# A hybrid attention and gMLP layer on one core: the gate's transpose copied out of PSUM by the scalar engine, the key's transpose moved beside the query's

## The chip, the cores and the metric

The kernel runs on one core of a Trainium2 chip. The metric is the device time of one execution in microseconds. Engines are named as in the profile: PE (matrix products and transposes), DVE (vector engine), ACT (scalar engine), POOL (GpSimd) and SP, which here issues most of the transfers.

## The reference

One layer works on `x` of 4096 tokens by 1024 channels, all float32:

```
h = rms(x) * (1 + scale) + shift
q, k, v, g_attn, u, v_gm, g_gm = split(h @ w_in)
attn = windowed_gqa(q, k, v)            # +-128 tokens, 8 query heads on 2 key heads, ALiBi, sink
gm   = chunked_gmlp(u, v_gm)            # chunks of 128 tokens
y = concat([attn * silu(g_attn), gm * silu(g_gm)])
x = x + gate * (y @ w_out)
```

The change lies in `attn * silu(g_attn)`, and in the transposes of `k` and `q` that the scores need.

## The kernel before

The sequence is cut into 32 blocks of 128 tokens. Matrix products keep float32 accuracy by splitting each operand into a high and a low part and adding three products, so that every block costs 24 products for keys and values (`pk`, 256 columns), 24 for queries (`pq`, 512) and 24 for the gate (`pg`, 512). After a short start the first part of the program is a loop (L782) over iterations i = 3 to 34. `run_iter` (L684) walks through the main products of block i in the order `pk`, `pq`, `pg` (`mains1`, L186) and puts side steps among them, at positions between 0 and 1 that the table `TUNE` (L36 to L40) and `sides1` (L635 to L682) give; of equal positions the one added first comes first. The attention of block a = i - 3 is among the side steps. A second part computes the gMLP branch and the output product; the change does not touch it.

The table sets the order in which the steps are written. The framework's scheduler then orders the instructions of each engine, and starts from the written order; only in iterations 29 to 31 (`chained`) are PE's pinned to it.

The steps that matter here, in the order of an iteration:

- `load1` and `split1` (L96, L97): SP loads the next blocks' `xraw` (transposed) and `xtok` (by tokens); ACT casts `xraw` to the high part `xh`, POOL computes the low part `xl`.
- `qk` (L538), one step for each head: two score products into a tile of pool "s" (`s`, names s_0 to s_7), a DVE instruction that adds the mask and takes the row minimum (L551, the minimum lands in `mx`), and ACT's exponential (L555). After four heads `softmax` (L559) takes the exponential of the sink (`es`, L566), the sum, its reciprocal, and POOL scales the rows (L571).
- `silu1` (L527): ACT's tanh of the gate into the one buffer `th` (L531), then DVE's product (L536).
- `stats1` (L164): ACT squares `xtok` and sums the rows, DVE and POOL make the reciprocal root (L82, L83).
- `pt_` (L573): four transposes of probabilities into a bank of pool "t" (`pT`), ACT's cast to `ph` (L580), DVE's rest `pl` (L581), which reads the bank again. An iteration has six: two groups of heads by three key blocks, named pT_0_0 to pT_1_2. `pv_` (L584): the products with the values (`po`), ACT's copy `lo` (L598) and DVE's sums into `y` (L600).
- `tr_g` (L607): four transposes of the gate into a bank of pool "s" (`gT`). `finish1` (L602): DVE multiplies `y` by it (L604) and SP stores the result.
- `post_kv`, `post_q`, `post_g` (L432, L453, L493): DVE takes the products out of PSUM (`kvf` L437, `qf` L457, `gf` L495), ACT squares (L440, L460), DVE reduces (L467), POOL takes the power (L83), DVE multiplies (L470, L485, L491, L486).
- `tr_k` (L498) and `tr_q` (L508) for block i - 1: the transposed keys `pkT` into pool "t", with casts `kT` (L504, L505) and the rest (L506); the queries `pqT` into pool "s", with `qT` (L518, L519).

PSUM has four pools of two banks each (L108): "mm" for the main products, "s" for scores, `gT` and `pqT`, "t" for `pT` and `pkT`, "o" for `po`. The buffers of a pool are given out in turn, so a tile waits for the last reader of the tile that held its bank.

Of the kernel before, what the change touches and what calls it, by code (L numbers as in the profile page):

```python
# [8 lines left out]
F32 = mybir.dt.float32  # L9
# [7 lines left out]
P = 128  # L17
# [19 lines left out]
            "v2"], ["v3", "g2", "g3"]], wg0=1.05, wgd=0.18, vn=0, vx=0.2, wv0=0.145, wvd=0.15,  # L37
            silu=0.45, ksplit=2, sb=["q1", "g0", "g1", "q0", "q2", "g2"], ch0=28, load=0.02, split=0.0,
            stats=0.525, bg=0.1, qk0=0.08, qkd=0.035, pt0=0.485, ptd=0.0715, pvlag=0.31, trg=0.5,
            fin=0.99, trk=0.93, trq=0.9, order="kqg", unch=0, hp2=30, hpx=0, qeng="V")  # L40


def body(tc, x, xT, c, cT, w_adaT, b_adaT, w_gate, b_gate, ngT, w_in, q_gain, k_gain, sink, wsT, bsT, w_out, out):
    nc = tc.nc
    V, A, G, T = nc.vector, nc.scalar, nc.gpsimd, nc.tensor
# [17 lines left out]
    def tr(ps, src):  # L63
        pe(T.transpose(ps, src, ident))  # L64
# [56 lines left out]
    base = ctx.enter_context(tc.tile_pool(name="base", bufs=1))  # L121
# [485 lines left out]
    def tr_g(b):  # L607
        d = blk[b]
        pt = ps_s.tile([P, 4, P], F32, tag="s", name=f"gT{b}")
        for i in range(4):  # L610
            tr(pt[:, i], d["gf"][:, i * P : (i + 1) * P])
        d["pg"] = pt

    def bg_bias2(n):
        k, t = divmod(n, 3)
# [19 lines left out]
    def sides1(i):  # L635
# [17 lines left out]
        if 0 <= a < NB:  # L653
            for b in range(NB):
                if i == max(b + LAG - 1, NS):
                    add(TUNE["silu"] if b > 1 else 0.0, lambda b=b: silu1([b]))
            _, s0, s1 = slots(a)
            for h in range(NH):
                add(TUNE["qk0"] + TUNE["qkd"] * h, lambda h=h: qk(a, h))
            seq = [(j, q) for j in range(NKV) for q in range(s0, s1)]  # L660
            for n, (j, q) in enumerate(seq):
                add(TUNE["pt0"] + TUNE["ptd"] * n, lambda j=j, q=q: pt_(a, j, q))
                add(TUNE["pt0"] + TUNE["ptd"] * n + TUNE["pvlag"], lambda j=j, q=q: pv_(a, j, q))
            add(TUNE["trg"], lambda: tr_g(a))
            add(max(TUNE["fin"], TUNE["pt0"] + TUNE["ptd"] * 5 + TUNE["pvlag"] + 0.001), lambda: finish1(a))
# [535 lines left out]
```

## Time and profile before

| what | value |
|---|---|
| three runs | 1730.27, 1732.02 and 1732.11 us, median 1732.02 |
| the profiled execution | 1732.1 us, its span 1730.3 us |
| PE busy | 1661.7 us, 96% of the span |
| DVE, ACT, POOL busy | 1075.7, 738.7, 689.4 us |
| granted TensorE clock, mean over the span | 0.987 of full speed |
| the loop over blocks | steady from about 115 to 706 us, then a tail to about 870 us |

The span is the stretch that the profiler saw; the execution's time also has what lies around it, here 1.8 us. Busy time overlaps between engines. A wait of an engine is listed with the instruction that waited and the one that ended the wait; that of an engine off the critical path costs nothing.

### The profile page before, as it was taken

How to read it: one execution, taken by the hardware profiler on the slowest of the kernel's cores; microseconds unless marked ns; L12 is line 12 of the kernel's file. 1: busy time of each engine (PE TensorE's matmuls, PEld its weight loads, DVE VectorE, ACT ScalarE, POOL GpSimd, SP SyncE). 2: the span in 40 equal slices, each digit the busy share in tenths (PEclk: the TensorE clock that was granted, in tenths of full speed). 3: DMA queues.
4: the chain of work that ended last, by engine and by line, in shares of the span. 5: the costliest groups of instructions: out<-in, count | busy, mean ns of one | idle time of the engine just before them, and what ended most of it. 6: DMA issues, size and time to landing. Idle time of an engine off the chain costs nothing.

```text
span 1730.3 us, 23014 instructions
## 1 busy us (share of the span) xinstructions
PE 1661.7 (96%) x8216; PEld 1377.6 (80%) x8216; DVE 1075.7 (62%) x2279; ACT 738.7 (43%) x1613; POOL 689.4 (40%) x610
## 2 busy tenths in 40 slices
PE   6789999999999999998989999999999989999999
PEld 4578888888888888886778888887888877888887
DVE  7987777787777778779773333344443466444443
ACT  3476666666666666665421212211122233222221
POOL 5653343433344433336522222222222337545552
PEclk9899999999999999999999999999999999999999
DMA  7522112222112222122250111213233146555442
GB/s 257 195 86 74 57 54 74 74 74 74 48 63 74 73 74 80 35 70 79 75 183 30 49 37 49 84 69 116 104 116 97 56 166 216 165 164 180 150 149 83
DMA packets 67762, 170.92 MB, mean 99 GB/s; under 512 B 8256, under 2 KB 8256, under 8 KB 67648
## 3 DMA queue, kind: packets, MB, share of 16 engines
q1 hardware_dynamic: 62896, 160.81, 27.8%
q10 hardware_dynamic: 4752, 8.65, 1.3%
q8 instruction: 64, 1.05, 0.2%
q14 instruction: 50, 0.41, 0.1%
HBM read 128.54 MB, written 40.89 MB: 98 GB/s over the span
## 4 chain that ended last, share of the span: by engine, by line
PE 76%; DVE 11%; DMA 2%; ACT 2%; issue 1%; POOL 1%; SPq 0%; DVEq 0%; POOLq 0%; ACTq 0%
PE pg L61 16%; PE pv L61 9%; PE pq L61 9%; PE pu L61 8%; PE oY L967 7%; PE oZ L967 5%; PE oX L967 5%; PE s L61 4%; PE pT L64 4%; PE po L61 3%; DVE y L600 3%; DVE pr L551 1%; PE sv L61 1%; PE pk L61 1%; DVE gf L495 1%
## 5 line engine op out<-in xcount | busy, mean ns | idle before, releaser
L97 POOL TENSOR_TENSOR xl<-xraw,xh 128x1024 fp32r<-128x1024 f32 x58 | 149.8, 2582 | 366.7 <-ACT xh L96 366.7
L571 POOL TENSOR_SCALAR pr<-pr,den 128x384 f32<-128x384 f32 (+1 forms) x256 | 146.4, 591 | 162.4 <-DVE vs L445 119.0
L555 ACT ACTIVATE pr<-pr,mx 128x384 f32<-128x384 f32 (+1 forms) x256 | 153.8, 601 | 61.0 <-DVE mx L551 60.2
L551 DVE CUSTOM_DVE_ANT_0 pr<-s,negd,nsink 128x384 f32<-128x384 f32 (+1 forms) x256 | 152.5, 607 | 11.7 <-PE s L61 6.2
L580 ACT CAST ph<-pT 128x512 fp32r<-128x512 f32 x188 | 109.6, 584 | 115.7 <-PE po L61 43.0
L61 PE MATMUL pu<-w2u,xh 128*128 128x512 f32 x480 | 149.2, 392 | 0.0
L61 PE MATMUL s<-kT,qT 128*128 128x384 f32 (+1 forms) x512 | 136.4, 348 | 12.8 <-DVE mx L551 11.0
L581 DVE TENSOR_TENSOR pl<-pT,ph 128x512 fp32r<-128x512 f32 x188 | 126.0, 685 | 15.6 <-ACT ph L580 15.6
L83 POOL TENSOR_TENSOR ssv<-ssv,mhalf 128x8 f32<-128x8 f32 x32 | 54.3, 1696 | 183.3 <-DVE ssv L82 183.1
L64 PEld LDWEIGHTS pT<-ident,pr 128*128 128x128 f32 x752 | 93.3, 140 | 34.8 <-POOL pr L571 6.8
L64 PE MATMUL pT<-ident,pr 128*128 128x128 f32 x752 | 115.7, 274 | 5.2 <-DVE pl L581 3.5
L61 PEld LDWEIGHTS s<-kT,qT 128*128 128x128 f32 x512 | 87.3, 190 | 32.9 <-DVE mx L551 19.5
L61 PEld LDWEIGHTS pu<-w2u,xh 128*128 128x128 f32 x480 | 90.9, 189 | 18.8
L96 ACT CAST xh<-xraw 128x1024 fp32r<-128x1024 f32 x61 | 64.1, 1050 | 91.1 <-PE pu L61 89.0
L61 PE MATMUL pg<-wgh,xl 128*128 128x512 f32 x232 | 98.7, 425 | 0.0
L61 PE MATMUL pg<-wgh,xh 128*128 128x512 f32 x232 | 98.5, 424 | 0.0
L61 PE MATMUL pu<-w2u,xl 128*128 128x512 f32 x240 | 94.2, 392 | 1.2 <-DVE xl L97 1.2
L61 PE MATMUL pq<-w1h,xh 128*128 128x512 f32 x232 | 94.2, 406 | 0.0
L61 PE MATMUL pq<-w1l,xh 128*128 128x512 f32 x232 | 93.9, 405 | 0.0
L61 PE MATMUL pq<-w1h,xl 128*128 128x512 f32 x232 | 92.0, 396 | 0.0
L61 PE MATMUL pg<-wgl,xh 128*128 128x512 f32 x232 | 91.8, 396 | 0.0
L230 DVE SCALAR_TENSOR_TENSOR vf<-pv,rstd,bias 128x512 f32<-128x512 f32 x32 | 24.0, 750 | 108.9 <-PE pv L61 108.8
(337 smaller groups left out, 4511.4 us busy)
## 6 DMA issues: line engine op xcount, KB each, us to landing
xraw<-xT SPq DMA_DIRECT2D x61, 512.0 KB, 3.9
xtok<-x SPq DMA_DIRECT2D x32, 512.0 KB, 5.1
yr<-yT SPq DMA_DIRECT2D x64, 256.0 KB, 4.3
xt<-x SPq DMA_DIRECT2D x32, 512.0 KB, 3.8
out<-xt SPq DMA_DIRECT2D x64, 256.0 KB, 3.5
wada<-w_adaT SPq DMA_DIRECT2D x16, 512.0 KB, 5.7
yT<-ybuf ACTq DMA_DIRECT2D x32, 256.0 KB, 2.2
yT<-y SPq DMA_DIRECT2D x31, 256.0 KB, 5.2
```

What stands on the lines that cost most here:

```text
L61: pe(T.matmul(ps, lhsT, rhs, start=start, stop=stop))
L64: pe(T.transpose(ps, src, ident))
L83: G.tensor_tensor(dst, dst, mhalf[:, :width], ALU.pow)
L96: A.copy(xh, xr)
L97: ins = eng.tensor_tensor(xl, xr, xh.bitcast(F32), ALU.subtract)
L551: V.tensor_tensor_reduce(flat(t[:, s0:s1]), flat(pss[:, s0:s1]), flat(negd[:, b % 3, s0:s1]), -(2.0 ** -(h + 1)), nsink[:, h : h + 1], ALU ...
L555: A.activation(t, t, AF.Exp, bias=m[:, i : i + 1], scale=-1.0, accum_out=d["den", j][:, i : i + 1])
L571: G.tensor_scalar(t, t, den[:, i : i + 1], 1.0, ALU.mult, ALU.mult)
L580: A.copy(ph, pt)
L581: V.tensor_tensor(pl, pt, ph.bitcast(F32), ALU.subtract)
L600: V.tensor_tensor(d["y"][e * HD : (e + 1) * HD, 2 * j : 2 * j + 2], po[:HD, e::2], lo[:, e::2], ALU.add)
L967: pe(T.matmul(ps, l[:, k], r[k], start=i < 3 and k == 0 and j == 0, stop=k == KC // 2 - 1 and j == 2, skip_group_check=i >= 3))
```

## The change

The key's transposes get the position of the query's, 0.9, and since `tr_k` is added first, it is written just ahead of them. `tr_g` copies the transposed gate from PSUM into an SBUF tile `gTs` on ACT, right after the transposes; this tile has the tag of the tanh's `th`, which has one buffer, so the two take turns in it. `finish1` then multiplies by the copy. Lines behind L612 move by one.

```diff
--- before.py
+++ after.py
@@ -37,7 +37,7 @@
             "v2"], ["v3", "g2", "g3"]], wg0=1.05, wgd=0.18, vn=0, vx=0.2, wv0=0.145, wvd=0.15,
             silu=0.45, ksplit=2, sb=["q1", "g0", "g1", "q0", "q2", "g2"], ch0=28, load=0.02, split=0.0,
             stats=0.525, bg=0.1, qk0=0.08, qkd=0.035, pt0=0.485, ptd=0.0715, pvlag=0.31, trg=0.5,
-            fin=0.99, trk=0.93, trq=0.9, order="kqg", unch=0, hp2=30, hpx=0, qeng="V")
+            fin=0.99, trk=0.9, trq=0.9, order="kqg", unch=0, hp2=30, hpx=0, qeng="V")
 
 
 def body(tc, x, xT, c, cT, w_adaT, b_adaT, w_gate, b_gate, ngT, w_in, q_gain, k_gain, sink, wsT, bsT, w_out, out):
@@ -609,7 +609,8 @@
         pt = ps_s.tile([P, 4, P], F32, tag="s", name=f"gT{b}")
         for i in range(4):
             tr(pt[:, i], d["gf"][:, i * P : (i + 1) * P])
-        d["pg"] = pt
+        d["pg"] = base.tile([P, 4, P], F32, tag="th", name=f"gTs{b}", bufs=1)
+        A.copy(d["pg"], pt)
 
     def bg_bias2(n):
         k, t = divmod(n, 3)
```

What the scheduler makes of it stands in the order of the engines' instructions, here for the iteration of block 17, which holds the attention of block 14 (the numbers behind a name are the block, then the head or group).

First ACT, from the fifth exponential of block 14 (pr14_4) and the Square of `xtok` to the square of `qf` (sq17). Before:

```order
L555 ACTIVATE pr14_4_4868,den14_1_4864<-pr14_4_4868,mx14_1_4863 128x384
L164 ACTIVATE xtok20_5076,rstd_134<-xtok20_5076 128x1024
L555 ACTIVATE pr14_5_4876,den14_1_4864<-pr14_5_4876,mx14_1_4863 128x384
L555 ACTIVATE pr14_6_4884,den14_1_4864<-pr14_6_4884,mx14_1_4863 128x384
L555 ACTIVATE pr14_7_4892,den14_1_4864<-pr14_7_4892,mx14_1_4863 128x384
L566 ACTIVATE es14_1_4895<-es14_1_4895 128x4
L580 CAST ph14_0_0_4922<-pT14_0_0_4917 128x512
L580 CAST ph14_0_1_4943<-pT14_0_1_4938 128x512
L460 ACTIVATE sq17_4854<-qf17_4949 128x512
```

and now:

```order
L164 ACTIVATE xtok20_5106,rstd_134<-xtok20_5106 128x1024
L555 ACTIVATE pr14_4_4896,den14_1_4892<-pr14_4_4896,mx14_1_4891 128x384
L555 ACTIVATE pr14_5_4904,den14_1_4892<-pr14_5_4904,mx14_1_4891 128x384
L555 ACTIVATE pr14_6_4912,den14_1_4892<-pr14_6_4912,mx14_1_4891 128x384
L555 ACTIVATE pr14_7_4920,den14_1_4892<-pr14_7_4920,mx14_1_4891 128x384
L566 ACTIVATE es14_1_4923<-es14_1_4923 128x4
L580 CAST ph14_0_0_4950<-pT14_0_0_4945 128x512
L613 COPY gTs14_4959<-gT14_4954 128x512
L580 CAST ph14_0_1_4973<-pT14_0_1_4968 128x512
L460 ACTIVATE sq17_4882<-qf17_4979 128x512
```

The Square has moved from behind the fifth exponential to ahead of it, and the copy `gTs14` stands between the first and the second `ph` cast.

Second PE, at the end of the iteration, from the first value products of block 14 (po14_0) on: the transposes of the queries (pqT16) and of the keys (pkT16) of block 16. Before:

```order
L61 MATMUL po14_0_4998<-pl14_0_1_4944,vs13_3722 128x512
L61 MATMUL pg17_4782<-wgl5_187,xh17_4499 128x512
L61 MATMUL pg17_4782<-wgh5_186,xl17_4500 128x512
L64 MATMUL pqT16_5019<-ident_131,qf16_4665 128x128 x4
L61 MATMUL pg17_4782<-wgh6_188,xh17_4499 128x512
L61 MATMUL pg17_4782<-wgl6_189,xh17_4499 128x512
L64 MATMUL pkT16_5030<-ident_131,kvf16_4571 128x128
L61 MATMUL pg17_4782<-wgh6_188,xl17_4500 128x512
L61 MATMUL po14_0_4998<-ph14_0_2_4966,vs14_4006 128x512
L61 MATMUL po14_0_4998<-pl14_0_2_4967,vs14_4006 128x512
```

and now:

```order
L61 MATMUL po14_0_5028<-pl14_0_1_4974,vs13_3742 128x512
L61 MATMUL pg17_4810<-wgl5_187,xh17_4525 128x512
L61 MATMUL pg17_4810<-wgh5_186,xl17_4526 128x512
L64 MATMUL pkT16_5048<-ident_131,kvf16_4597 128x128
L64 MATMUL pqT16_5057<-ident_131,qf16_4693 128x128 x4
L61 MATMUL pg17_4810<-wgh6_188,xh17_4525 128x512
L61 MATMUL pg17_4810<-wgl6_189,xh17_4525 128x512
L61 MATMUL pg17_4810<-wgh6_188,xl17_4526 128x512
L61 MATMUL po14_0_5028<-ph14_0_2_4996,vs14_4028 128x512
L61 MATMUL po14_0_5028<-pl14_0_2_4997,vs14_4028 128x512
```

The key's transpose has moved ahead of the query's four, past two products of `pg`.

Third PE, from the first score pair of block 14 (s14_0) on. Before, nine products of `pk` stand between the pairs s14_0 and s14_1, of which these are the last rows and what follows:

```order
L61 MATMUL pk17_4780<-w1h5_170,xl17_4500 128x256
L61 MATMUL pk17_4780<-w1h6_172,xh17_4499 128x256
L61 MATMUL s14_1_4816<-kT0_0_201,qT14_4450 128x384
L61 MATMUL s14_1_4816<-kT0_1_202,qT14_4450 128x384
L61 MATMUL pk17_4780<-w1l6_173,xh17_4499 128x256
L61 MATMUL pk17_4780<-w1h6_172,xl17_4500 128x256
L61 MATMUL pk17_4780<-w1h7_174,xh17_4499 128x256
L61 MATMUL s14_2_4826<-kT0_0_201,qT14_4450 128x384
L61 MATMUL s14_2_4826<-kT0_1_202,qT14_4450 128x384
```

and now four, with s14_2 behind four more:

```order
L61 MATMUL s14_0_4831<-kT0_1_202,qT14_4484 128x384
L61 MATMUL pk17_4808<-w1l3_167,xh17_4525 128x256
L61 MATMUL pk17_4808<-w1h3_166,xl17_4526 128x256
L61 MATMUL pk17_4808<-w1h4_168,xh17_4525 128x256
L61 MATMUL pk17_4808<-w1l4_169,xh17_4525 128x256
L61 MATMUL s14_1_4844<-kT0_0_201,qT14_4484 128x384
L61 MATMUL s14_1_4844<-kT0_1_202,qT14_4484 128x384
L61 MATMUL pk17_4808<-w1h4_168,xl17_4526 128x256
L61 MATMUL pk17_4808<-w1h5_170,xh17_4525 128x256
L61 MATMUL pk17_4808<-w1l5_171,xh17_4525 128x256
L61 MATMUL pk17_4808<-w1h5_170,xl17_4526 128x256
L61 MATMUL s14_2_4854<-kT0_0_201,qT14_4484 128x384
```

Counted from s14_0, the second pair has moved up by five products (9 to 4), the third by four (12 to 8), the fourth by one (14 to 13).

## Rows read from the trace of the kernel before

**Rows 1.** The page, part 1: busy time, share of the span, and instructions of each engine.
```profile
PE 1661.7 (96%) x8216; PEld 1377.6 (80%) x8216; DVE 1075.7 (62%) x2279; ACT 738.7 (43%) x1613; POOL 689.4 (40%) x610
```

**Rows 2.** Busy time in a stretch of steady iterations (PE, PEld, DVE, ACT, POOL; clock, DMA).
```profile
300.00:500.00 200.00, 197.94 (x1126) 170.76 (x1125) 159.98 (x424) 132.99 (x331) 78.04 (x89) 1.00 0.20 67
```

**Rows 3.** The waits of PE: total us, times, longest.
```profile
PE s L61 <- DVE mx L551: 11.0, 30, 2.6
...
PE pT L64 <- DVE pl L581: 3.5, 3, 2.3
```

**Rows 4.** PE's timeline: start us, us, engine, line, operation, out<-in, count [idle before <-releaser].
```profile
398.53 0.28 PE L61 MATMUL pk<-w1h,xh 128*128 128x256 f32 x1
...
422.71 0.28 PE L61 MATMUL pk<-w1h,xh 128*128 128x256 f32 x1
...
448.71 0.28 PE L61 MATMUL pk<-w1h,xh 128*128 128x256 f32 x1
449.16 0.62 PE L61 MATMUL s<-kT,qT 128*128 128x384 f32 x2 [0.17 <-DVE mx L551]
449.61 0.28 PE L61 MATMUL pk<-w1l,xh 128*128 128x256 f32 x1
...
466.11 0.60 PE L64 MATMUL pqT<-ident,qf 128*128 128x128 f32 x4
...
467.02 0.27 PE L64 MATMUL pkT<-ident,kvf 128*128 128x128 f32 x1
...
783.05 0.62 PE L61 MATMUL s<-kT,qT 128*128 128x384 f32 x2 [2.63 <-DVE mx L551]
```

**Rows 5.** DVE's timeline, a late iteration (410.00) and the iteration of block 17.
```profile
410.00 0.75 DVE L627 SCALAR_TENSOR_TENSOR bias<-bgw,shift,bias 128x512 f32<-128x512 f32 x1 [2.25 <-DMA bgw<-w_in]
...
449.02 0.08 DVE L551 DVE_READ_ACCUMULATOR2_ANT mx<- 128x1 f32 x1
449.02 0.68 DVE L604 TENSOR_TENSOR y<-y,gT 128x512 f32<-128x512 f32 x1
...
458.67 0.69 DVE L581 TENSOR_TENSOR pl<-pT,ph 128x512 fp32r<-128x512 f32 x1 [0.23 <-ACT ph L580]
459.45 0.75 DVE L457 SCALAR_TENSOR_TENSOR qf<-pq,rstd,bias 128x512 f32<-128x512 f32 x1
...
465.71 1.28 DVE L581 TENSOR_TENSOR pl<-pT,ph 128x512 fp32r<-128x512 f32 x2
```

**Rows 6.** ACT's timeline, the iteration of block 17 up to the next `xh`.
```profile
445.93 1.05 ACT L96 CAST xh<-xraw 128x1024 fp32r<-128x1024 f32 x1
...
454.98 1.06 ACT L164 ACTIVATE xtok<-xtok 128x1024 f32<-128x1024 f32 x1 [0.96 <-DMA xtok<-x]
...
456.04 0.60 ACT L555 ACTIVATE pr<-pr,mx 128x384 f32<-128x384 f32 x1
...
457.84 0.19 ACT L566 ACTIVATE es<-es 128x4 f32<-128x4 f32 x1
...
460.24 0.64 ACT L460 ACTIVATE sq<-qf 128x512 f32<-128x512 f32 x1 [0.66 <-DVE qf L457]
...
467.33 0.26 ACT L504 CAST kT<-pkT 64x128 fp32r<-64x128 f32 x1
...
468.02 0.58 ACT L598 COPY lo<-po 64x512 f32<-64x512 f32 x1 [0.17 <-PE po L61]
468.51 0.58 ACT L518 CAST qT<-pqT 64x512 fp32r<-64x512 f32 x1
...
469.56 1.05 ACT L96 CAST xh<-xraw 128x1024 fp32r<-128x1024 f32 x1
```

**Rows 7.** Groups by form: busy us, mean ns of one, idle before (ACT, then DVE).
```profile
L858 ACT COPY ybuf<-yT 128x512 f32<-128x512 f32 x32 | 18.0, 588 | 60.3 <-PE yT L64 52.1 <-DMA yT<-ybuf 8.2
...
L491 DVE TENSOR_TENSOR qf<-qf,ss 128x512 f32<-128x512 f32 x32 | 22.1, 691 | 0.0
...
L604 DVE TENSOR_TENSOR y<-y,gT 128x512 f32<-128x512 f32 x32 | 21.8, 681 | 0.0
```

## The prediction

> **What bounds the kernel now.** I read the engines' shares first: TensorE (PE) is busy for 96% of the span, the vector engine (DVE) for 62%, the scalar engine (ACT) for 43% [rows 1]. Then the stretches: from 300 to 500 us PE is busy 197.94 of 200 us [rows 2], so a cheaper instruction elsewhere gains nothing by itself; only PE's waits and its own work count. Then the list of PE's waits: the largest is that of score products on the row minimum (`mx`), 11.0 us in 30 places; waits on `pl` are 3.5 us in 3 [rows 3].
>
> The timeline shows where these 30 lie. In the iteration of block 17 (attention of block 14) PE runs a product of `pk` at 448.71, then stands until 449.16, when the second score pair (s_1) starts, 0.06 after `mx` of the first is read out (449.02 + 0.08); the next `pk` starts at 449.61 [rows 4, 5]. That is 0.90 for what takes some 0.46 without a wait (a `pk` product has a pitch of 0.11; for a pair I take 0.35): 0.44 us lost per iteration. The cause is in the code: pool "s" has two banks, and one holds gT from its transposes until DVE's product L604, 449.02 to 449.70 [rows 5], so s_1 has to reuse the bank of s_0. An iteration's period is 23.63 us: `xh` starts at 445.93 and again at 469.56 [rows 6].
>
> **The change, part by part.**
>
> *The copy on ACT* adds 32 copies of 128x512 from PSUM. The same shape costs 588 ns at L858 [rows 7]: 32 x 0.588 = 18.8 us of ACT. In the new order it stands behind the first `ph` cast and ahead of the second (first place of the section on the change). There ACT idles 0.66 before the square of `qf` at 460.24, waiting for DVE [rows 6], so the copy fits and I cost it at nothing. If that cover were gone, the price would be up to 0.59 per iteration. A copy ahead of a product could be repaid by a cheaper product: L604 with a PSUM operand takes 681 ns, L491 of the same shape with both operands in SBUF 691 [rows 7], so DVE gains nothing. The Trainium skill (VectorE: DVE Perf Modes, Rules for kernel authors) says that elementwise work on matmul output should be done from PSUM, or copied out first only if many operations will use it; here one does, the rows agree, and by that rule alone the copy is 18.8 us of ACT for nothing but the bank.
>
> *The bank.* gT gives its bank back after the copy, ten us before s_0. Then s_1 waits for no reduction, s_2 for `mx` of s_0, s_3 for that of s_1. PE is 0.44 earlier, up to s_3. But mx_1 stands behind mx_0, L604 (pitch 0.59) and its own reduction (0.6): 1.2 us after mx_0. PE reaches s_3 two pairs and four products of `pk` later than it reached s_1 (third place): 2 x 0.35 + 4 x 0.11 = 1.15. So the wait carries over to s_3 almost whole, unless DVE itself gets earlier.
>
> *The tanh* shares its buffer with the copy, so it must follow L604; it now stands behind the first exponential, one block later, where ACT waits for `mx` anyway: nothing.
>
> *The key transpose (K)* moves from behind two `pg` products to just ahead of the query's. Its bank is the one that the subtraction `pl` of the fifth probability transpose (pl_1_1) reads. That is the first of the two at 465.71; two take 1.28, one 0.69 [rows 5], so it ends near 466.40, and 0.06 later K may start: 466.46. The query's transposes started at 466.11 [rows 4]. So K stalls PE by 0.35 us, where before, at 467.02, it had 0.56 to spare. Behind it stand the query's transposes, the last `pg` and `po` products and the next block; on ACT the key casts, then `qT`, then `xh`. Likewise the first cast of this group can start at 466.46 + 0.31 = 466.77, where the query's could at 466.11 + 0.60 = 466.71: DVE's chain through `kT`, `qT`, `y`, `gf` to s_0 starts 0.06 later. As s_3 hangs on it, the period by this loop is 23.63 + 0.06 = 23.69.
>
> *The Square of `xtok`* on ACT now stands ahead of the fifth exponential instead of behind it (first place). It waits for its DMA and starts 9.05 us after `xh`, at 454.98 [rows 6], 0.96 of this idle. That wait is now in front of all four exponentials. The loop that this closes:
> - `xh` to Square: 454.98 - 445.93 = 9.05. In it lie `xl` on POOL, the issue of both loads on SP (`xraw` waits for `xl`) and the flight; none is touched.
> - Square to the first exponential 1.06 (456.04); four at 0.60 (three took 456.04 to 457.84): 2.40.
> - the sum's exponential to the first `pl`: 457.84 to 458.67 = 0.83. `pl` to `qf`: 1.28 - 0.69 = 0.59.
> - `qf` to pl_1_1: 459.45 to 465.71 = 6.26, through the square, the reduction, POOL's power and three products. pl_1_1 and the signal: 0.69 + 0.06.
> - K to the next `xh`: 0.31 to the first cast (467.02 to 467.33), then kT, kT, qT, kT, kT, lo, qT. Lo with qT, kT, kT behind it took 468.02 to 469.56 = 1.54; qT, kT, kT 468.51 to 469.56 = 1.05. Together 2.90.
>
> The sum is 9.05 + 3.46 + 0.83 + 0.59 + 6.26 + 0.75 + 2.90 = 23.84 [rows 5, 6], longer than 23.63 and than 23.69. In the kernel before, the fourth exponential was not in the loop, and `qf` waited for the last `pq` product, not for ACT, so there it was no limit. I take +0.21 us for the 24 iterations whose Square stands so (attention of blocks 2 to 25): **+5.0 us**. Bounds: +0.06 (Square loop covered: +1.4), and +0.31 if the first `pl` takes its whole 0.69 instead of the pitch (+7.4).
>
> That such a delay isn't swallowed shows in one iteration of the kernel before: a late weight load held DVE by 2.25 us at 410.00 ahead of the exponential sum; that iteration lasted from 398.53 to 422.71, 24.18 [rows 4, 5], 0.55 more than the others.
>
> *Ends.* In the tail PE waits 2.63 us for `mx` at 783.05 [rows 4], with DVE behind POOL; the freed bank moves this from one score pair to a later one. I take nothing, between -3 (gone) and +3 (a second one like it).
>
> **Sum**: the profiled execution took 1732.1 us, the median of the runs is 1732.02, so the same base. 1732.1 + 5.0 = **1737.1 us**, its own range 1733 to 1741.
>
> **The rivals.**
> - *The bubble goes and nothing takes its place* (faster): 0.44 x 24 = 10.6 us off, **1721.5**. For it: it is the largest of PE's waits [rows 3] and its cause, the bank, is removed; PE has little else to wait for [rows 2]. The Trainium skill (Perfetto Trace Analysis, Optimization Strategy) says that a bubble repeated on the engine that should be saturated can mean too little SBUF or PSUM for the next tile, and this change gives just that. Against it: DVE's chain isn't shortened. It decides if mx_1 comes 0.44 earlier against K than the sum has it, and if the four exponentials have 0.2 us of slack that I don't see.
> - *Only DVE's loop counts* (no change): the load of `xtok` lands early enough, as all transfers shift together. Then 23.69: +1.4, **1733.5**. For it: the Square's excess is 0.15 us over this loop, less than one instruction. Against: the load is issued behind `xl`, so it moves with `xh`.
> - *Worse*: the late group also stalls the transposes behind POOL's scaling, and the waits at K, at these and at s_3 add rather than overlap. If the fifth exponential's whole 0.60 is paid, 0.60 x 24 = 14.4: **1746.5**. The late iteration, at 0.55, speaks for it; that `xh` comes only 2.90 behind K, with fewer products between, speaks against.
> - That the change does not do what it says can be left out: the order shows the copy, and K ahead of the query's.
>
> **How the numbers follow.** Square loop 0.50, bubble gone 0.20, DVE's loop alone 0.22, worse 0.08. A difference under 0.2% (3.5 us) can hardly be told from none. Of the Square loop's share about 0.33 lies above +3.5 us and 0.17 within; of DVE's loop 0.03 above, 0.16 within and 0.03 below; the worse case is all above, the bubble's all below but 0.01. Slower 0.44, same 0.34, faster 0.22. The range reaches from 1727 (a bubble half gone) to 1743, which leaves out most of the fast rival and most of the worst case.
>
> **What would show it.** Right: in steady iterations PE no longer waits at s_1 but at K for `pl`, about 0.3 us each, some 24 times, and at s_3 for `mx`; the Square still starts 9.0 after `xh` and four exponentials follow it; the period is 23.8. Wrong: PE waits under 2 us in all on `mx` and `pl`, or a period at or under 23.6; or a copy that ends after `qf`, so that the second `ph` is late.

## The result and the profile after

The changed kernel takes 1744.25 us (median of six runs), the kernel before 1731.26: a ratio of 1.0075, 95% interval 1.0063 to 1.0087. It is slower, as forecast, but by 13 us where 5 were forecast, and 1.25 us above the range. The profiled execution has a span of 1743.0 us, 12.7 more than before.

The page, part 1, and the waits of PE (total us, times, longest) of the changed kernel:

```profile
PE 1669.0 (96%) x8216; PEld 1368.2 (78%) x8216; DVE 1066.4 (61%) x2279; ACT 749.4 (43%) x1645; POOL 688.7 (40%) x610
```

```profile
PE pkT L64 <- DVE pl L581: 8.6, 28, 1.4
PE s L61 <- DVE mx L551: 8.1, 8, 2.7
```

Against [rows 3] the score products no longer wait in every iteration (8 places, not 30); the key's transpose does, in 28. That is the exchange that the prediction described. Its size stands in ACT's timeline (first fence; the iteration from 524.02) and in those of PE and DVE (second and third), which answer to [rows 4 to 6]:

```profile
524.02 1.05 ACT L96 CAST xh<-xraw 128x1024 fp32r<-128x1024 f32 x1
...
533.14 1.06 ACT L164 ACTIVATE xtok<-xtok 128x1024 f32<-128x1024 f32 x1 [1.58 <-DMA xtok<-x]
...
534.20 0.60 ACT L555 ACTIVATE pr<-pr,mx 128x384 f32<-128x384 f32 x1
...
536.60 0.19 ACT L566 ACTIVATE es<-es 128x4 f32<-128x4 f32 x1
536.82 0.59 ACT L580 CAST ph<-pT 128x512 fp32r<-128x512 f32 x1
537.30 0.60 ACT L613 COPY gTs<-gT 128x512 f32<-128x512 f32 x1
537.77 0.61 ACT L580 CAST ph<-pT 128x512 fp32r<-128x512 f32 x1
...
538.82 0.64 ACT L460 ACTIVATE sq<-qf 128x512 f32<-128x512 f32 x1 [0.43 <-DVE qf L457]
...
545.40 0.26 ACT L504 CAST kT<-pkT 64x128 fp32r<-64x128 f32 x1 [0.68 <-PE pkT L64]
...
545.95 0.58 ACT L518 CAST qT<-pqT 64x512 fp32r<-64x512 f32 x1
546.56 0.26 ACT L504 CAST kT<-pkT 64x128 fp32r<-64x128 f32 x1
...
548.08 1.05 ACT L96 CAST xh<-xraw 128x1024 fp32r<-128x1024 f32 x1
```

```profile
545.03 0.33 PE L64 MATMUL pkT<-ident,kvf 128*128 128x128 f32 x1 [0.25 <-DVE pl L581]
```

```profile
537.43 0.69 DVE L581 TENSOR_TENSOR pl<-pT,ph 128x512 fp32r<-128x512 f32 x1 [0.23 <-ACT ph L580]
538.04 0.74 DVE L457 SCALAR_TENSOR_TENSOR qf<-pq,rstd,bias 128x512 f32<-128x512 f32 x1
...
544.30 1.28 DVE L581 TENSOR_TENSOR pl<-pT,ph 128x512 fp32r<-128x512 f32 x2
...
551.42 0.75 DVE L604 TENSOR_TENSOR y<-y,gTs 128x512 f32<-128x512 f32 x1
```

From `xh` to `xh` it takes 24.06 here; the median of 24 iterations is 23.99, against 23.63 before. Where the 12.7 us of span lie, by the starts of the first `pk` product of each block in PE's timeline:

| stretch | before | after | difference |
|---|---|---|---|
| up to block 4 | 114.91 | 113.08 | -1.8 |
| iteration of block 4 | 23.68 | 26.81 | +3.1 |
| 24 iterations, blocks 5 to 28 | 567.59 | 576.69 | +9.1 |
| two iterations in pinned order | 48.39 | 49.88 | +1.5 |
| the rest | | | +0.8 |

### The profile page after: what moved, and what is told of

The parts are those of the page before. It is cut to its first block, busy times and chain, and to the rows that moved or that the text cites. A ratio compares the mean times of both kernels' runs of the same rounds, so it can differ in the third digit from the quotient of the medians.

```text
span 1743.0 us, 23075 instructions
## 1 busy us (share of the span) xinstructions
PE 1669.0 (96%) x8216; PEld 1368.2 (78%) x8216; DVE 1066.4 (61%) x2279; ACT 749.4 (43%) x1645; POOL 688.7 (40%) x610
## 4 chain that ended last, share of the span: by engine, by line
PE 47%; DVE 5%; POOL 2%; issue 1%; DMA 1%; ACT 1%; SPq 0%; DVEq 0%; POOLq 0%; ACTq 0%
PE pv L61 9%; PE pg L61 9%; PE pu L61 8%; PE oY L968 7%; PE oZ L968 5%; PE oX L968 5%; PE sv L61 1%; PE yT L64 1%; DMA stT<-wB_T 1%; POOL ssv L83 1%; DVE gate L871 1%; PE pT L64 1%; PE po L61 0%; DVE ug L832 0%; DVE pr L551 0%
## 5 line engine op out<-in xcount | busy, mean ns | idle before, releaser
L61 PE MATMUL pv<-w2vh,xh 128*128 128x512 f32 x224 | 90.8, 405 | 0.0
```

The lines of the kernel that those rows point to most:

```text
L61: pe(T.matmul(ps, lhsT, rhs, start=start, stop=stop))
```

## The experiments

"Period" is the median of the 24 iterations, from the same starts. The edits are shown shortened, with remarks added. A Square is held in its place on ACT by a helper that adds an order without a wait:

```diff
+    def behind(ins, other):
+        tc.add_manual_dep(ins.ins, other.ins.name, ..., reason="order")
```

| run | us | ratio to before, 95% | period |
|---|---|---|---|
| changed kernel | 1744.25 | 1.0063 to 1.0087 | 23.99 |
| copy alone | 1742.71 | 1.0051 to 1.0081 | 23.98 |
| key's transpose alone | 1799.60 | 1.0376 to 1.0407 | 26.33 |
| changed, Square two blocks late | 1761.64 | 1.0162 to 1.0192 | 24.55 |
| changed, load order turned | 1749.69 | 1.0090 to 1.0131 | 23.99 |
| changed, Squares back | 1738.84 | 1.0028 to 1.0058 | 23.80 |
| before, Squares ahead | 1739.34 | 1.0028 to 1.0058 | 23.96 |
| copy alone, Squares back | 1738.10 | 1.0024 to 1.0047 | 23.85 |
| changed, Squares in ACT's gap | 1741.52 | 1.0037 to 1.0071 | 23.85 |
| and product later | 1734.88 | 1.0010 to 1.0030 | 23.59 |
| and key's transpose behind | 1727.39 | 0.9958 to 0.9981 | 23.33 |
| and block 7's Square in the gap | 1726.61 | 0.9966 to 0.9987 | 23.33 |

**The copy alone.** Against the changed kernel:

```diff
-            fin=0.99, trk=0.9, trq=0.9, ...
+            fin=0.99, trk=0.93, trq=0.9, ...
```

> The changed kernel with the key's transpose back behind the two products (position 0.93), the copy kept. ACT's order keeps the Square of xtok ahead of the fifth exponential. Theory (the loss is a loop that needs both: the Square ahead of the fifth exponential, and the key's transpose at the head of the last group): the loop is then 9.06 + 3.46 + 0.83 + 0.61 + 6.25 + 0.75 to the earliest key transpose and 2.54 from it to xh (467.02 to 469.56 in the kernel before), 23.50, and no longer limits. PE waits at the fourth score pair instead of the second, a period of 23.6 to 23.7, about 1731 to 1734 us. Rival A (the Square's place, or the copy, costs its delay by itself): the period stays near 23.95 and the time at 1741 to 1745.

1742.71 us: a miss for the theory, and what rival A said. In the steady part the key's transposes no longer wait (two waits are left, outside it), and the period is 23.98, against 23.99 in the changed kernel. So the key's place was not what closed the loop.

**The key's transpose alone.** The same edit of the number, the other way, in the kernel before.

> The kernel before with only the key's transpose moved to 0.9, no copy. In ACT's order three exponentials stand behind the Square, as before. Theory (loop): 9.06 + 2.86 + 0.83 + 0.61 + 6.25 + 0.74 + 3.05 = 23.40, no limit; the key's transpose waits for pl 0.2 to 0.35 us per iteration, and the second score pair still waits for the row minimum; period 23.7, about 1732 to 1736 us. Rival B (the key's wait is paid in full, whatever the Square does): 0.31 x 24 = 7.4 more than before, 1738 to 1741.

1799.60 us, far from both. The scheduler made another order out of it: the second score pair stands 12 products behind the first, and PE waits in 27 places for the gate's product, which holds the bank, and in 82 for POOL:

```profile
PE s L61 <- DVE y L604: 24.4, 27, 0.9
PE pT L64 <- POOL pr L571: 19.9, 82, 1.2
```

It prices no single move. It shows that positions in the table can't be undone one by one here; from there on instructions were held in place.

**The Square behind the fifth exponential, first try.** The hold was tied to the attention block that is written beside the Square (block b - 4):

```diff
+        behind(sq, blk[b - 4]["mark"])    # mark: the fifth exponential
```

> The changed kernel with the Square of xtok held behind the fifth exponential on ACT, as it stood before the change; everything else is that of the change. Theory (loop through the Square): the loop loses one exponential, 23.99 - 0.60 = 23.39, and DVE's chain to the fourth score pair is next at 23.7; 0.29 x 24 = 7 us come back, 1735 to 1738 us. Rival B (the key's wait by itself): the time stays at 1742 to 1746.

1761.64 us. The order before had the Square of block b beside the attention of block b - 6; this held it two blocks later than meant, so its buffer came free late and the load of the next `xtok` waited for it (issued 9.2 us after `xh` instead of 3.9). The key's transpose then waited 23.8 us for `pl`, in 27 places; the way from the load to that wait was not followed. The run says nothing on the question.

**The load of `xtok` first.**

```diff
-        d["xr"] = load_xT(ap, b)
-        load_tok(b)
+        load_tok(b)
+        d["xr"] = load_xT(ap, b)
```

> The changed kernel with the load of xtok issued ahead of that of xraw, so that it no longer waits for the low part of xh on POOL, and the Square no longer for the load (its order on ACT then comes out behind the sixth exponential). Theory (loop through the load): the 9.06 us from xh to the Square are gone, the Square waits for no load; what is left is DVE's chain, 23.7: 1735 to 1738 us as with the Square held behind, with a late load no longer passed on. Rival B: 1742 to 1746.

1749.69 us. The load did not come earlier: SP issued it 4.89 us after `xh` (3.94 in the changed kernel), behind a weight load and the store of `y`. The Square started at 10.22 in place of 9.06, but only two exponentials stood behind it:

```profile
501.94 1.05 ACT L96 CAST xh<-xraw 128x1024 fp32r<-128x1024 f32 x1
...
512.16 1.06 ACT L164 ACTIVATE xtok<-xtok 128x1024 f32<-128x1024 f32 x1 [1.47 <-DMA xtok<-x]
...
514.42 0.19 ACT L566 ACTIVATE es<-es 128x4 f32<-128x4 f32 x1
```

10.22 + 1.06 + 2 x 0.60 = 12.48 to `es`, in the changed kernel 9.12 + 1.06 + 4 x 0.60 = 12.58, its median 12.52; and the period is 23.99 in both. It is `es` that the period follows here, not the Square. Of the 5.4 us that this run is slower, 2.0 lie in the 24 iterations of the profiled execution, which has two with a late load (25.82 and 25.13); the rest was not traced.

**Only the Squares back.** The hold tied to the right block. Counted over all engines, 24 instructions of ACT change places with one neighbour each, nothing else moves.

```diff
+        behind(sq, blk[b - 6]["mark"])    # b > 7, mark: the fifth exponential
```

> The changed kernel with the 24 Squares of blocks 8 to 31 behind the fifth exponential of the same iteration on ACT, as before the change; no other instruction of any engine moves. Theory (the Square's place delays the four exponentials by one, 0.60 us, and the time follows es): es comes 11.9 after xh in place of 12.5, the loop through K is 23.39 and DVE's chain, at 23.7, is next: 24 x 0.29 = 7 us come back, 1736 to 1738 us. Rival B (the key's wait in front of the query's transposes is the loss): 1743 to 1745.

1738.84 us, period 23.80: 24 x 0.19 = 4.6 of the 5.4 us between the medians, a little less than expected. What is left over 23.63 is DVE's chain, for which PE now stands twice: the fourth pair starts 0.28 after the product ahead of it, where 0.12 is usual, and the key's transpose 0.57, where 0.24 is usual (medians). In the kernel before, it stood once, 0.47 to the second pair where 0.11 is usual. DVE's and PE's timelines in this run:

```profile
499.20 0.62 DVE L556 CUSTOM_DVE_ANT_0 pr<-s,negd,nsink 128x384 f32<-128x384 f32 x1
499.74 0.08 DVE L556 DVE_READ_ACCUMULATOR2_ANT mx<- 128x1 f32 x1
499.74 0.75 DVE L611 TENSOR_TENSOR y<-y,gTs 128x512 f32<-128x512 f32 x1
500.42 0.60 DVE L556 CUSTOM_DVE_ANT_0 pr<-s,negd,nsink 128x384 f32<-128x384 f32 x1
500.95 0.07 DVE L556 DVE_READ_ACCUMULATOR2_ANT mx<- 128x1 f32 x1
```

```profile
501.08 0.61 PE L61 MATMUL s<-kT,qT 128*128 128x384 f32 x2
```

The fourth pair starts at 501.08, 0.06 after the second minimum is read out (500.95 + 0.07): the wait has moved from the second pair to the fourth, as forecast.

**Only the Squares, in the kernel before.** The counterpart: no copy, no moved transpose.

```diff
+        behind(blk[b - 6]["mark"], sq)    # the fifth exponential behind the Square
```

> The kernel before with its 24 Squares of blocks 8 to 31 ahead of the fifth exponential on ACT, as after the change; no copy, no moved transpose, no other instruction moves. Theory (time follows es, whichever way it reaches the next xh): es 12.5 after xh, the last pl 0.4 later, DVE's chain to the second score pair with it, a period of 23.9 to 24.0: 1738 to 1742 us. Rival C (a delay of the exponentials costs only where K stands ahead of the query's transposes, as the prediction had it): the loop is 23.5, the time stays at 1730 to 1733.

1739.34 us, period 23.96: the loss of the whole steady part, in a kernel that has nothing else of the change. Rival C, the prediction's own view, is out. The way by which the delay reaches the next `xh` without the key's transposes stands in DVE's, PE's and ACT's timelines:

```profile
557.95 0.69 DVE L588 TENSOR_TENSOR pl<-pT,ph 128x512 fp32r<-128x512 f32 x1 [0.23 <-ACT ph L587]
```

```profile
558.31 0.39 PE L61 MATMUL pg<-wgl,xh 128*128 128x512 f32 x1
558.70 0.66 PE L64 MATMUL pT<-ident,pr 128*128 128x128 f32 x4
...
566.08 0.27 PE L64 MATMUL pkT<-ident,kvf 128*128 128x128 f32 x1
```

```profile
544.76 1.05 ACT L96 CAST xh<-xraw 128x1024 fp32r<-128x1024 f32 x1
...
553.67 1.06 ACT L168 ACTIVATE xtok<-xtok 128x1024 f32<-128x1024 f32 x1 [1.42 <-DMA xtok<-x]
...
568.62 1.05 ACT L96 CAST xh<-xraw 128x1024 fp32r<-128x1024 f32 x1
```

The third probability transpose starts at 558.70, 0.06 after the first `pl` ends (557.95 + 0.69) and 0.39 after the product ahead of it, where 0.23 is usual: pool "t" has two banks, and it needs the one that the first `pl` reads. From there PE runs without a stop: 7.38 to the key's transpose, 2.54 more to `xh`. With 8.91 to the Square, 4.28 from it to that `pl` and 0.75 for `pl` and the signal this is 23.86, this iteration's length.

**The copy alone, Squares back.**

> The copy without the moved key transpose (as the run with the copy alone), and the 24 Squares back behind the fifth exponential. What the copy does by itself, without its effect on the Square. Theory: the wait at the second score pair is gone and that at the fourth is as long; period 23.6 to 23.7, with the start of the run with the copy alone (about 2 to 3 us late): 1733 to 1736 us. Rival D (the freed bank pays once the Square is out of the way): 1721 to 1727.

1738.10 us, period 23.85: over the expected range, and rival D is out. The wait is as frequent as in the kernel before ([rows 3]: 11.0 us in 30 places) and longer, though it is now that of the fourth pair:

```profile
PE s L61 <- DVE mx L556: 11.6, 30, 2.8
```

The groups by form show what got longer on DVE ahead of it: the product of `y` and the gate, in the kernel before, in this run and in the last but one of the table:

```profile
L604 DVE TENSOR_TENSOR y<-y,gT 128x512 f32<-128x512 f32 x32 | 21.8, 681 | 0.0
```

```profile
L611 DVE TENSOR_TENSOR y<-y,gTs 128x512 f32<-128x512 f32 x32 | 30.5, 952 | 0.0
```

```profile
L613 DVE TENSOR_TENSOR y<-y,gTs 128x512 f32<-128x512 f32 x32 | 22.9, 715 | 0.0
```

**The Squares in ACT's gap.** Held behind the fourth `ph` cast, where ACT idles.

```diff
+        behind(sq, blk[b - 6]["mark"])    # b > 7, mark: the cast ph of the second group's first
```

> The changed kernel with the 24 Squares between the fourth and the fifth ph cast on ACT, where ACT idles some 1.2 us in every iteration; the root that follows on DVE and POOL moves with them. Theory: no exponential waits for the load any more, es comes by 11.9 or earlier; what is left is DVE's chain, 23.7, as with the Squares back in their place: 1735 to 1738 us, and a late load is no longer passed on. If the place behind the fifth exponential still held the loop, this run is the faster of the two.

1741.52 us, over the expected range, period 23.85: no faster than with the Squares back, so behind the fifth exponential they no longer held the loop. The 0.05 that the period is longer lie on DVE: the root's first instruction (L82) now stands just ahead of the last two `pl`, at 540.31 and 540.37, and the key's transpose, which waits for the first of them, starts 0.62 after the product ahead of it, not 0.57:

```profile
540.31 0.15 DVE L82 TENSOR_SCALAR rstd<-rstd 128x1 f32<-128x1 f32 x1
540.37 1.28 DVE L588 TENSOR_TENSOR pl<-pT,ph 128x512 fp32r<-128x512 f32 x2
```

**The product later.**

```diff
+        behind(blk[b - 1]["fin"], red)    # fin: y * gTs, red: the reduction of the second head
```

> The run with the Squares in the gap (period 23.85, fourth score pair waiting for the second reduction), and besides the product of y and the copied gate held behind that second reduction on DVE (it stood between the first and the second), possible only because the copy has freed the bank; the tanh then follows the second exponential. Theory (what is left at 23.8 is DVE's chain through the product and the second reduction to the fourth score pair): the reduction is 0.7 us earlier, PE no longer waits there; the key transpose still waits for pl some 0.33 us, so the period is 23.2 + 0.3 = 23.5, and the time 1741.5 - 24 x 0.35 = 1731 to 1735 us. Rival E (the chain at 23.8 is that of the key casts alone, or ACT's): the time stays at 1739 to 1742.

1734.88 us, period 23.59, near what was expected. With the product, the tanh, DVE's product with it and one product of `pq` change places in each iteration. DVE's chain through the product was what remained; in the steady part the key's transposes alone now make PE wait:

```profile
PE pkT L64 <- DVE pl L590: 8.7, 28, 1.4
```

**And the key's transpose behind.**

> The same with the key's transpose back behind the two products (position 0.93): copy, Squares in the gap, product behind the second reduction. Theory: neither the fourth score pair nor the key's transpose makes PE wait; the period comes near PE's own work of 23.2, 23.2 to 23.35, and the time to 1723 to 1729 us, under the kernel before. Rival E: DVE's chain still ends last and the period is over 23.6, 1733 or more.

1727.39 us, as expected, 0.9970 of the kernel before. PE is busy 199.67 of 200 us in the steady part ([rows 2]: 197.94):

```profile
310.00:510.00 200.00, 199.67 (x1137) 171.62 (x1136) 158.35 (x423) 135.62 (x337) 86.65 (x98) 1.00 0.20 67
```

Against the run before it the key's place is worth 0.26 us per iteration, and 1.8 us in the two pinned ones (49.85 and 48.09).

**One more Square.**

> The previous run (copy, key's transpose behind, Squares in the gap, product behind the second reduction), and one more Square, that of block 7, held behind the cast of the fourth probability transpose: in the first full iteration (block 4) it stands ahead of the third exponential of the first group, and all kernels with the copy lose 2.5 to 3.1 us there (26.2 to 26.8 us in place of 23.7). Theory (again a Square that waits for its load in front of exponentials): that iteration comes to 23.5 to 24.5, 2 to 2.5 us come back, 1724 to 1726 us. Rival F (that iteration is long because the keys and queries of blocks 0 to 2 come late from the start): it stays at 26.2, 1727 to 1728.

1726.61 us. The iteration of block 4 falls from 26.19 to 25.07, half of what was expected, and PE's listed waits in it from 1.6 to 0.7 us (for POOL's scaled rows). So the Square explains a part of that iteration's loss; whether rival F explains the rest was not tried. The time itself can't show 1.1 us: the ratios of the two runs, 0.9970 and 0.9977, have intervals that overlap.

## Why the prediction was wrong in size

The direction was right. Two terms of the sum were too small, and the loop was tied to a condition that it doesn't need.

*The copy on ACT is hidden*: right. It stands at 537.30 between two `ph` casts, and ACT still waits 0.43 for DVE behind them.

*DVE gains nothing from the copy*: wrong, it loses. The prediction took L491's 691 ns for a product from SBUF; L604 went from 681 to 746 ns, and to 952 where the key's transpose stayed behind. L491 stands where POOL computes nothing; this product stands at the end of `xl`. The section on the hardware has the rows.

*The wait moves from the second pair to the fourth*: right (501.08). *DVE's chain costs 0.06*: mis-sized. With the Squares back the period is 23.80, +0.17. The first `kT` cast starts 0.37 behind the key's transpose, not 0.31, from that cast to the product it is 6.02 (545.40 to 551.42), not the 5.90 of before, and the product's pitch is 0.68 instead of 0.59, which has no row behind it in the prediction.

*The key's transpose stalls PE by 0.35*: right in size, 8.6 us in 28 places, 0.31.

*The loop through the Square is 23.84*: right in its terms but for one. Medians near 9.06 + 3.46 + 0.83 + 0.61 + 6.25 + 0.74 stand against 9.05 + 3.46 + 0.83 + 0.59 + 6.26 + 0.75. From the key's transpose to `xh` it is 3.05 (545.03 to 548.08), not 2.90: the first cast comes later, and the first `qT` is followed after 0.61, not the 0.48 read from the second. This term was mis-sized, and it alone is 24 x 0.15 = 3.6 us.

*That this loop needs the key's transpose ahead*, "In the kernel before, the fourth exponential was not in the loop": this is the step of the mechanism that failed. The Squares alone give 23.96, the copy alone 23.98. Where the key's transposes don't wait, the third probability transpose does, for the bank of the first `pl`. By the medians both ways take 10.65 us from the start of that `pl` to the next `xh`: 0.61 + 6.25 + 0.74 + 3.05 with the key's transpose ahead, 0.75 + 7.36 + 2.54 with it behind (the run with the copy alone). That they are equal is chance. So in the steady part the move of the key's transpose cost nothing that the Squares had not cost already, and the loop came out near its length under a condition that it doesn't need. The sign of it was in the trace of before, in the late iteration that the prediction used; PE's timeline there:

```profile
412.45 0.33 PE L64 MATMUL pT<-ident,pr 128*128 128x128 f32 x1 [0.34 <-DVE pl L581]
```

*Ends at nothing, between -3 and +3*: they came to +3.6 (-1.8, +3.1, +1.5 and +0.8). The prediction looked at the tail for this. The -1.8 and the +0.8 can't be laid to the change: the kernel before and the run with the Squares ahead in it have the same order in these two stretches, and took 114.91 and 112.80 for the one, 975.76 and 977.65 for the other. The +1.5 and the +3.1 come back in other runs. The two iterations in pinned order last 49.85 to 49.91 in the six kernels with the copy and the key's transpose ahead, and 48.09 to 48.11 in the four with the copy and it behind, so this is the key's place. Of the +3.1 in the iteration of block 4, 2.5 are there with the copy alone (26.14); a Square that waits for its load stands ahead of six exponentials there, which the last run shows to be a part of it.

*A late load*, at worst 1.0 us (Square at 461.10, period 25.01), is passed on in full, because it is in the loop. The 24 iterations lost 9.1 where 24 x 0.36 are 8.6; with the forecast's 5.0, the last term's 3.6 and the ends' 3.6, these 0.5 make up the 12.7 us. So the time left the range by two terms of the sum, the way from the key's transpose to `xh` and the ends; either alone would have left it inside (1737.1 + 3.6 = 1740.7).

By cause the steady part's 9.1 us can't be split in one way. Putting the Squares back takes 4.9 of them off (576.69 to 571.75 for the 24 iterations), and leaves 4.2 for the longer DVE chain and the key's place; but the Squares alone, in the kernel before, cost 8.5 (576.11 against 567.59). The two losses overlap. The faster rival failed for the reason given against it. Its other condition, a shorter DVE chain, was the way to the version that beats both.

## What to carry to other kernels

A freed buffer moves a wait; it removes it only if the engine that releases the next buffer is earlier too, so follow that engine's chain to the next place and shorten it there. Compare the whole order of every in-order engine after such an edit: an unrelated instruction that waits for a transfer may have slipped ahead of urgent ones. Where a delay enters a loop, list all ways back to its start, each buffer with two banks among them, before calling any of them covered.

## What the runs showed of the hardware

A DVE product with both operands in SBUF and POOL's `xl` hold each other up: the one that starts later is held. A product with an operand in PSUM was not. POOL's `xl` and DVE's product in the run with the copy alone and the Squares back:

```profile
521.59 2.41 POOL L97 TENSOR_TENSOR xl<-xraw,xh 128x1024 fp32r<-128x1024 f32 x1 [6.24 <-ACT xh L96]
```

```profile
523.53 1.01 DVE L611 TENSOR_TENSOR y<-y,gTs 128x512 f32<-128x512 f32 x1
```

They overlap by 0.47 us, and the product takes 1.01: it ends 0.54 after `xl`. In the changed kernel `xl` (549.21 to 551.62) overlaps by 0.20, and the product takes 0.75: it ends 0.55 after `xl`. With the product held behind the second reduction it starts after `xl` ends, and takes 0.69:

```profile
537.33 2.40 POOL L97 TENSOR_TENSOR xl<-xraw,xh 128x1024 fp32r<-128x1024 f32 x1 [4.19 <-ACT xh L96]
```

```profile
539.81 0.69 DVE L613 TENSOR_TENSOR y<-y,gTs 128x512 f32<-128x512 f32 x1
```

In the kernel before, `xl` (447.06, 2.39 long) overlapped the product from PSUM by 0.43, which still took 0.68 [rows 5]. Its second part has the long overlap and the other order, in a product of two SBUF tiles:

```profile
895.38 2.38 POOL L97 TENSOR_TENSOR xl<-xraw,xh 128x1024 fp32r<-128x1024 f32 x1 [2.66 <-ACT xh L96]
...
920.43 2.85 POOL L97 TENSOR_TENSOR xl<-xraw,xh 128x1024 fp32r<-128x1024 f32 x1 [7.78 <-ACT xh L96]
```

```profile
895.83 2.49 DVE L831 TENSOR_TENSOR ug<-ug,gfm 128x512 f32<-128x512 f32 x1
...
920.34 0.69 DVE L831 TENSOR_TENSOR ug<-ug,gfm 128x512 f32<-128x512 f32 x1
```

The first of these products overlaps `xl` by 1.93 us, takes 2.49, and again ends 0.55 or 0.56 after it; the second starts 0.09 ahead of `xl`, keeps its 0.69, and `xl` takes 2.85 instead of 2.39. The Trainium skill (SBUF — State Buffer, SBUF: two separate sides) says that DVE and GpSimd share one pair of ports, an exclusive lock that whichever starts first keeps for the whole instruction, and that a DVE instruction with two SBUF inputs needs it against a GpSimd one that reads SBUF. The rows agree: in all three overlaps the product, 0.69 alone, ends some 0.55 after `xl`, so that all but about its first 0.14 us waits. This rule spoke against the change, and the prediction did not weigh it.
